# S5 fed by a planned clock, more modulation chunks beside it, four rotation tables made early: one core, two hybrid layers

## The chip, the cores and the metric

The kernel runs on one core of a Trainium2 chip. The metric is the device time of one execution in microseconds (us); before the change the median of three runs is 3060.22 us, the lowest 3058.78 us and the highest 3065.08 us. A profiled execution was taken apart from these.

## The reference

One inference step of a two-layer backbone over 128 context tokens and 128 latent tokens, with D = 2048, all in fp32. Each layer, cut to what matters:

```python
mod = silu(cond) @ w_mod[l] + b_mod[l]             # 6 vectors of 2048, for context and latent
h = rms_norm(x) * (1 + scale1) + shift1
q, k, v, xr, xg, us, gl = split(h @ w_in)          # gl: three gates of 2048
attn = block_attention(rope(norm(q)), rope(norm(k)), v)         # 8 heads, 2 kv heads
rec  = gelu(xg) * rg_lru_bidir(conv4(xr))                       # 1024 channels
ssm  = s5_bidir(us); ssm = gelu(ssm); ssm *= sigmoid(ssm @ glu_w)   # 64 groups, 64 complex states, 2 directions
merged = g0 * (attn @ w_pa) + g1 * (rec @ w_pr) + g2 * (ssm @ w_ps)
x = x + gate1 * (merged @ w_o)
a, b = split((rms_norm(x) * (1 + scale2) + shift2) @ w_up)
x = x + gate2 * ((gelu(conv3(a)) * b) @ w_down)
```

The S5 branch is a linear recurrence with complex coefficients, h[t] = A h[t-1] + B u[t], run forward and backward. The outputs are x of both token sets, the context's k and v, and the final states.

## The kernel before, in words

**Units.** All weights come from DRAM as half-tiles of 512 KB, called `raw` (a ring of six buffers, loaded by SP). fp32 products are made from two parts: ACT casts a half-tile to `whi` (`acp`, L114) and DVE subtracts to get `wlo` (L70). A unit is one 128-column output of a 2048-row product: two half-tiles, 32 matmuls on PE into `ps_mm` (L117); then ACT copies one half of the result and DVE adds the other (`pj`). So each unit asks DVE for two `wlo` of 128x1024 and one `pj` of 128x256.

**Items.** `run_items` walks a list: units ("w"), single steps ("do") and modulation loads ("mod"). A layer's list is: w_us, q, k, v, xr (the columns of w_in), then w_pa with the gate of the attention branch and the xg columns, then w_pr with its gates, the S5's glu, w_ps, w_o, and the FFN. Layer 0's w_us and half of its q are made in a startup stage beside the first norm.

**Modulation chunks.** The products with w_mod for later vectors are filler. `filler(n)` adds `MODR[seg]` per unit to a credit, and whenever this reaches 4 it puts a chunk of four w_mod half-tiles into the list. A chunk is four loads of 512 KB and 16 narrow matmuls into `ps_md` (two records each in the trace), with no split, so nothing for DVE or ACT but a small end. The six entries of `MODR` stand for six stretches of the program in turn.

**What runs beside the units.** Attention, the RG-LRU and the S5 are Python generators, and each `next` emits one step. `feed` (L215), called after every unit, steps them: attention four steps a unit (`RATT`), LRU 1.9, and the S5 by a budget of planned DVE time per unit, `RS5` = 4.2 us in layer 0 and 2.6 us in layer 1, cut to `SATT` = 2.2 and 1.5 us while attention runs. The planned cost of a DVE instruction is 150 or 90 ns plus a rate by its size.

**The S5.** Eight tiles, two directions each, so 16 passes a layer (`s5_gen`). A pass on DVE is two products `pa` and `pb` of PE's `ps_v` with a table of rotations, two sums into `xs`, a scan (L1001), two products back (`pc`, `pd`) and two sums into `H`. The table and the other coefficients of a tile stand in the buffer `blk` (two of them) and are made by `s5_prep` (L831) on DVE: the coefficients `S` and `cc`, and the table by six doublings. Layer 0's tiles 0 and 1 are prepared in the startup by `prep_step`, two steps per eighth of it; tiles 2 to 7 inside the S5 of layer 0. Layer 1's eight are prepared during layer 0's FFN and kept in DRAM (`s5a`, `s5v`).

**Order.** Each engine executes its instructions in the order that the framework's scheduler writes. It works from the order of emission, its own estimate of times and the free buffers. A buffer is named by its tag: `t` (products p1/p2 of the preparation), `S`, `xs`, `RH` and `H` have one buffer each or a pair.

Of the kernel before, what the change touches and what calls it, by code (L numbers as in the profile page):

```python
# [33 lines left out]
class Builder:  # L34
    RS5 = (4.2, 2.6)
    HLB = 3
    GS0 = 10
    PATIENCE = 3
    NRAW = 6
    AHEAD = 20  # L40
    MODR = (0.94, 0.94, 0.9, 0.9, 0.9, 1.44)
    RATT = (4.0, 4.0)
    RLRU = (1.9, 1.9)
    SATT = (2.2, 1.5)
# [209 lines left out]
    def run_items(self):  # L254
# [26 lines left out]
        for i in range(n):  # L281
# [15 lines left out]
            else:  # L297
# [21 lines left out]
                self.feed(1.0)  # L319
# [109 lines left out]
    def startup(self, begin, evs, begin2, evs2):  # L429
# [22 lines left out]
        prep = [self.s5_prep(0, 0), self.s5_prep(0, 1)]  # L452
# [58 lines left out]
        for q in range(8):  # L511
# [319 lines left out]
    def s5_prep(self, l, ft):  # L831
# [51 lines left out]
        self.add(cc[:, 1, 1], t1[:, 1], t2[:, 0])  # L883
        self.nc.vector.memset(tab[:, 0, :, 0:1], 1.0)
# [161 lines left out]
    def att_gen(self, l):  # L1046
        nc, d = self.nc, self.d
        Q, KV = self.Q, self.KVT
        KR, KA, VP, VS = (KV[n] for n in ("KR", "KA", "VP", "VS"))

# [19 lines left out]
        self.recip(sg, sg)  # L1070
        self.ts(sg, sg, float(P) ** -0.5, ALU.mult)
# [4 lines left out]
        qs = Q[:, :, P:T]  # L1076
        for g in range(3):
            n = 4 if g < 2 else 2
            src = qs[:, 4 * g:4 * g + 4, :] if g < 2 else KR[:, :, P:T]
            w = self.misc([4, P])  # L1080
            self.mm(w[:, 0:n, :], self.PERM, src, True, True)
            t1 = F1
            self.mul(t1[:, 0:n], src, self.COS[:, None, :].to_broadcast([P, n, P]))
            yield
            t2 = self.st("F2", [4, P], name="rt2")
            self.mul(t2[:, 0:n], w[:, 0:n], self.SIN[:, None, :].to_broadcast([P, n, P]))
            self.add(src if g < 2 else KA[:, :, P:T], t1[:, 0:n], t2[:, 0:n])
            yield
        for kv in range(2):
            for hh in range(4):  # L1090
                h = 4 * kv + hh
                s = self.misc([3, P])
                self.mm(s[:, 0, :], Q[:, h, 0:P], KR[:, kv, 0:P], True, True)
                self.mm(s[:, 1:3, :].rearrange("p a b -> p (a b)"), Q[:, h, P:T], KA[:, kv, :], True, True)
                yield
                sm = self.st("sm", [6], name="sm", bufs=2)
                nc.vector.tensor_reduce(sm[:, 0:1], s[:, 0, :], mybir.AxisListType.X, ALU.max)
                nc.vector.tensor_reduce(sm[:, 1:2], s[:, 1:3, :], mybir.AxisListType.XY, ALU.max)
                self.dve += 600
                sgh = sg[:, 2 * h:2 * h + 2]  # L1100
                self.stt(sm[:, 2:4], sm[:, 0:2], -1.0, sgh, ALU.mult, ALU.mult)
                p = F1[:, 0:3]
                self.act(p[:, 0, :], s[:, 0, :], AF.Exp, bias=sm[:, 2:3], scale=sgh[:, 0:1], accum=sm[:, 4:5])
                self.act(p[:, 1:3, :], s[:, 1:3, :], AF.Exp, bias=sm[:, 3:4], scale=sgh[:, 1:2], accum=sm[:, 5:6])
                yield
                self.recip(sm[:, 4:6], sm[:, 4:6])
                self.ts(p[:, 0, :], p[:, 0, :], sm[:, 4:5], ALU.mult)
                self.ts(p[:, 1:3, :], p[:, 1:3, :], sm[:, 5:6], ALU.mult)
                yield
                w = self.misc([3, P])  # L1110
                for j in range(3):
                    self.tr(w[:, j, :], p[:, j, :])
                yield
                self.acp(PT[:, :, hh, :], w)
            yield
            for s in range(2):
                o = self.misc([4, P])
                if s == 0:
                    self.mm(o, VP[:, kv * P:(kv + 1) * P], PT[:, 0], True, True)
                else:  # L1120
                    for j in range(2):
                        self.mm(o, VS[:, j, kv * P:(kv + 1) * P], PT[:, 1 + j], j == 0, j == 1)
                yield
# [7 lines left out]
    def lru_gen(self, l):  # L1131
        nc, d = self.nc, self.d
        XC = self.XC
        for k in range(8):
# [29 lines left out]
            for dd in range(2):  # L1164
                for s in range(2):
# [5 lines left out]
                    self.dve += 90 + 1.04 * P  # L1171
# [8 lines left out]
    def layer(self, l):  # L1180
# [71 lines left out]
        for g in range(2):  # L1252
            def mm(hv, g=g):
# [14 lines left out]
                if g == 1:  # L1268
                    def ev():
# [5 lines left out]
                        self.start(self.att, self.RATT[l], "att")  # L1275
# [343 lines left out]
def program(nc, shapes):  # L1619
# [30 lines left out]
```

## Time and profile before

| what | value |
|---|---|
| median of 3 runs | 3060.22 us |
| the profiled execution | 3068.35 us, its span 3066.6 us |
| PE (matmul) busy | 2952.2 us, 96% |
| PEld (weight load) busy | 2483.6 us, 81% |
| DVE busy | 2257.7 us, 74% |
| ACT busy | 1730.4 us, 56% |
| DMA read and written | 704.46 MB and 15.68 MB, 235 GB/s over the span |

The shares are of the span of the profiled execution. PE's share is an average over stretches in which it is nearly full and others in which it waits, so the table alone doesn't tell what a change in one stretch is worth. The stretches used below, in us from the span's start: 0 to 162 the startup; 162 to 307 the rest of q, k, v and xr of layer 0; 307 to 815 its w_pa and w_pr with gates; 815 to 1613 its glu, w_ps, w_o and FFN; 1613 to 2337 layer 1 up to its w_pr; 2337 to the end the rest of layer 1.

### The profile page before, as it was taken

How to read it: one execution, taken by the hardware profiler on the slowest of the kernel's cores; microseconds unless marked ns; L12 is line 12 of the kernel's file. 1: busy time of each engine (PE TensorE's matmuls, PEld its weight loads, DVE VectorE, ACT ScalarE, POOL GpSimd, SP SyncE). 2: the span in 40 equal slices, each digit the busy share in tenths (PEclk: the TensorE clock that was granted, in tenths of full speed). 3: DMA queues.
4: the chain of work that ended last, by engine and by line, in shares of the span. 5: the costliest groups of instructions: out<-in, count | busy, mean ns of one | idle time of the engine just before them, and what ended most of it. 6: DMA issues, size and time to landing. Idle time of an engine off the chain costs nothing.

```text
span 3066.6 us, 53452 instructions
## 1 busy us (share of the span) xinstructions
PE 2952.2 (96%) x20833; PEld 2483.6 (81%) x20833; DVE 2257.7 (74%) x4000; ACT 1730.4 (56%) x2914; POOL 45.9 (1%) x87
## 2 busy tenths in 40 slices
PE   6899999999999999999999999999999999999999
PEld 4787778777888888888887877777788888888888
DVE  6389899999576787787667788688755777666665
ACT  4355668745556745445566557676445567544553
POOL 0000000000000000000000000000000000000000
PEclk8999999999999999999999999999999999999999
DMA  9856566566777778778776777777776556555553
GB/s 382 306 183 203 177 208 218 196 208 236 263 262 253 251 282 286 273 270 291 266 275 241 267 250 252 244 259 250 261 278 202 178 175 208 197 187 192 181 197 132
DMA packets 188493, 723.64 MB, mean 236 GB/s; under 512 B 21520, under 2 KB 22064, under 8 KB 179280
## 3 DMA queue, kind: packets, MB, share of 16 engines
q1 hardware_dynamic: 180288, 689.86, 65.3%
q0 software_dynamic: 7664, 28.27, 2.5%
q8 instruction: 164, 2.69, 0.4%
q10 hardware_dynamic: 288, 2.10, 0.2%
q14 instruction: 89, 0.73, 0.1%
HBM read 704.46 MB, written 15.68 MB: 235 GB/s over the span
## 4 chain that ended last, share of the span: by engine, by line
PE 66%; DVE 14%; issue 9%; DMA 6%; ACT 5%; POOL 0%; DVEq 0%; ACTq 0%; SPq 0%; POOLq 0%
PE ps_mm L117 59%; DVE wlo L70 5%; DMA raw<-in_w_in 3%; PE ps_md L117 3%; ACT whi L114 2%; DVE xs L1001 2%; PE ps_aux L117 1%; PE ps_v L117 1%; DVE xs L70 1%; PE ps_y L117 1%; DVE t L70 1%; DVE pb L70 1%; DVE pj L70 1%; DMA raw<-in_w_mod 1%; DMA raw<-in_w_pr 1%
## 5 line engine op out<-in xcount | busy, mean ns | idle before, releaser
L117 PE MATMUL ps_mm<-h,whi 128*128 128x512 f32 (+1 forms) x4976 | 1743.9, 395 | 40.7 <-DVE pj L70 32.4
L70 DVE TENSOR_TENSOR wlo<-raw,whi 128x1024 fp32r<-128x1024 f32 x896 | 1095.3, 1223 | 449.4 <-ACT whi L114 444.7
L117 PE MATMUL ps_mm<-h,wlo 128*128 128x256 f32 x4912 | 1341.7, 283 | 17.1 <-DVE wlo L70 16.7
L114 ACT CAST whi<-raw 128x1024 fp32r<-128x1024 f32 x896 | 939.6, 1049 | 517.8 <-PE ps_mm L117 231.6
L117 PEld LDWEIGHTS ps_mm<-h,whi 128*128 128x128 f32 x4976 | 926.6, 190 | 254.1 <-DVE pj L70 39.7
L117 PEld LDWEIGHTS ps_mm<-h,wlo 128*128 128x128 f32 x4912 | 934.7, 190 | 44.6 <-DVE wlo L70 23.2
L114 ACT COPY pj<-ps_mm 128x256 f32<-128x256 f32 x479 | 176.1, 369 | 500.1 <-PE ps_mm L117 499.4
L117 PE MATMUL ps_mm<-hid,whi 128*128 128x512 f32 x1024 | 354.7, 393 | 0.0
L70 DVE TENSOR_TENSOR pj<-ps_mm,pj 128x256 f32<-128x256 f32 x479 | 200.9, 421 | 204.9 <-ACT pj L114 200.1
L117 PE MATMUL ps_mm<-br,whi 128*128 128x512 f32 x896 | 322.1, 402 | 12.3 <-DVE pj L70 12.3
L117 PE MATMUL ps_mm<-hid,wlo 128*128 128x256 f32 x1024 | 277.3, 281 | 0.0
L117 PE MATMUL ps_mm<-br,wlo 128*128 128x256 f32 x896 | 233.8, 281 | 0.0
L117 PEld LDWEIGHTS ps_mm<-hid,whi 128*128 128x128 f32 x1024 | 188.5, 188 | 39.5 <-issue 2.5
L117 PEld LDWEIGHTS ps_mm<-br,whi 128*128 128x128 f32 x896 | 165.4, 189 | 54.9 <-DVE pj L70 19.4
L117 PEld LDWEIGHTS ps_mm<-hid,wlo 128*128 128x128 f32 x1024 | 193.1, 189 | 5.4 <-DVE wlo L70 0.3
L117 PEld LDWEIGHTS ps_mm<-br,wlo 128*128 128x128 f32 x896 | 169.6, 189 | 8.4 <-ACT RH L110 0.4
L117 PE MATMUL ps_md<-raw,SC 128*32 128x256 f32 x2560 | 162.0, 381 | 0.0
L117 PEld LDWEIGHTS ps_md<-raw,SC 128*32 128x32 f32 x2560 | 82.9, 109 | 50.7 <-issue 12.6
L110 ACT ACT_TABLE_LOAD x90 | 115.5, 1283 | 10.3 <-DMA cv<-in_cT 5.0
L110 ACT ACTIVATE RH<-CST,TINY 128x256 f32<-128x256 f32 x128 | 57.2, 500 | 56.3 <-DVE xs L1001 56.1
L1001 DVE TENSOR_TENSOR_SCAN xs<-RH,xs 128x1056 f32<-128x1056 f32 x32 | 75.4, 2355 | 0.6
L83 DVE SCALAR_TENSOR_TENSOR x<-pj,MOD,x 128x128 f32<-128x128 f32 x192 | 59.0, 349 | 3.0
(239 smaller groups left out, 2448.4 us busy)
## 6 DMA issues: line engine op xcount, KB each, us to landing
raw<-in_w_mod SPq DMA_DIRECT2D x384, 512.0 KB, 6.9
raw<-in_w_in SPq DMA_DIRECT2D x304, 512.0 KB, 4.9
raw<-in_w_up SPq DMA_DIRECT2D x166, 512.0 KB, 4.4
raw<-in_w_up SPq DMA_DIRECT2D x45, 1024.0 KB, 4.9
raw<-in_w_down SPq DMA_DIRECT2D x90, 512.0 KB, 4.3
raw<-in_w_o SPq DMA_DIRECT2D x64, 512.0 KB, 4.4
raw<-in_w_down SPq DMA_DIRECT2D x19, 1024.0 KB, 4.9
raw<-in_w_pa SPq DMA_DIRECT2D x32, 512.0 KB, 4.6
```

The source lines that it names most:

```text
L70: self.nc.vector.tensor_tensor(out=out, in0=a, in1=b, op=op)
L83: self.nc.vector.scalar_tensor_tensor(out=out, in0=a, scalar=s, in1=b, op0=op0, op1=op1)
L110: self.nc.scalar.activation(out, a, func, **k)
L114: self.nc.scalar.copy(out, a)
L117: self.nc.tensor.matmul(out, lhsT, rhs, start=start, stop=stop, **k)
L1001: nc.vector.tensor_tensor_scan(out=x, data0=r, data1=x, initial=0.0, op0=ALU.mult, op1=ALU.add)
```

## The change

The S5 is no longer fed at a fixed rate. The planner now keeps a planned clock for DVE and one for PE; after every unit the S5 is stepped as long as DVE's clock is behind PE's plus `LEAD` (4.2 us in layer 0, 3.0 us in layer 1). The planned costs are closer to the measured ones (65 ns instead of 150 or 90). Attention takes one longer step per half unit, and within a kv head the scores of one head are emitted before the previous head's result is copied. `MODR` puts more chunks into the first stretch (1.5 instead of 0.94) and, per unit, fewer into the later ones. The rotation tables of layer 0's tiles 2 to 5 are made in the startup's list by `s5_tab_store`, in the buffers `xs`, `RH` and `H`, and stored by POOL to a DRAM tensor `s5t` (532 KB each); `s5_prep` then loads them by SP.

```diff
-    RS5 = (4.2, 2.6)
+    LEAD = (4200, 3000)
     HLB = 3
     GS0 = 10
+    NTAB = 4
     PATIENCE = 3
     NRAW = 6
     AHEAD = 20
-    MODR = (0.94, 0.94, 0.9, 0.9, 0.9, 1.44)
-    RATT = (4.0, 4.0)
+    MODR = (1.5, 0.6, 0.65, 0.65, 0.65, 1.2)
     RLRU = (1.9, 1.9)
-    SATT = (2.2, 1.5)
     NE = (3, 3)
     PA = 1
...
-        self.dve += 150 + 1.04 * out.free_size()
+        self.dve += 65 + 1.04 * out.free_size()
...
+        n, m = rhs.free_size(), lhsT.free_size()
+        if rhs.dtype == F32R:
+            self.pe += 7 + 0.443 * n
+        else:
+            self.pe += max(1.69 * n, 220) / (4 if m == 32 else 1)
...
+        self.tsplit = self.clock()
...
+        self.feed_att()
+
+    def clock(self):
+
+        self.dvet += self.dve - self.dve0
+        self.dve0 = self.dve
+        return self.dvet
+
+    def feed(self):
+
+        for g in sorted(self.gens, key=lambda g: g[3] == "s5"):
+            if g[3] == "att":
+                continue
             s5 = g[3] == "s5"
-            g[2] += w * (self.SATT[self.lay] if att and s5 else g[1])
+            g[2] = 0 if s5 else g[2] + g[1]
             if g[4] is not None:
                 g[4] += 1
-            while g[2] >= (0 if s5 else 1) and g in self.gens:
+            while g in self.gens and (self.clock() < self.pe + self.LEAD[self.lay] if s5 else g[2] >= 1):
                 if g[4] is not None and g[4] < self.PATIENCE:
-                    g[2] = min(g[2], 1.0)
                     break
-                t = self.dve
+                g[2] -= 1
                 self.step(g)
-                g[2] -= (self.dve - t) / 1e3 if s5 else 1
+
+    def feed_att(self):
+        for g in list(self.gens):
+            if g[3] == "att":
+                self.step(g)
...
-            if g[4] is not None:
+            if g[4]:
...
+                self.pe = max(self.pe, self.tsplit - 1200)
...
+                self.dvet = max(self.clock(), self.pe)
...
-                self.feed(1.0)
+                self.feed_att()
+                self.feed()
...
-        prep = [self.s5_prep(0, 0), self.s5_prep(0, 1)]
+        prep = [self.s5_prep(0, 0), self.s5_prep(0, 1)] + [self.s5_tab_store(2 + k) for k in range(self.NTAB)]
...
-            for _ in range(2):
+            for _ in range((2, 2, 3, 4, 5, 6, 7)[q - 1]):
                 self.do(prep_step)
         self.items += [us[7], qs[3]]
+        self.do(lambda: [0 for p in prep for _ in p])
...
+        if l == 0 and 2 <= ft < 2 + self.NTAB:
+            nc.sync.dma_start(tab.rearrange("p c d n -> p (c d n)"), d["s5t"][ft])
+            yield
+        else:
+            yield from self.s5_tab(tab, ft)
+
+    def s5_tab(self, tab, ft):
...
+    def s5_tab_store(self, ft):
+        t = self.st(("xs", "RH", "H")[ft % 3], [2, 8, 65], name="tb")
+        yield from self.s5_tab(t, ft)
+        self.nc.gpsimd.dma_start(self.d["s5t"][ft], t.rearrange("p c d n -> p (c d n)"))
...
-            for hh in range(4):
-                h = 4 * kv + hh
-                s = self.misc([3, P])
-                self.mm(s[:, 0, :], Q[:, h, 0:P], KR[:, kv, 0:P], True, True)
-                self.mm(s[:, 1:3, :].rearrange("p a b -> p (a b)"), Q[:, h, P:T], KA[:, kv, :], True, True)
+            for hh in range(5):
+                if hh:
+                    w = turn()
+                if hh < 4:
+                    s = scores(4 * kv + hh)
+                if hh:
+                    self.acp(PT[:, :, hh - 1, :], w)
...
-                    self.start(self.s5, self.RS5[l], "s5")
+                    self.start(self.s5, 0, "s5")
...
-                        self.start(self.att, self.RATT[l], "att")
+                        self.start(self.att, 1.0, "att")
```

What moves on the engines, from the order in which they execute. First DVE at the end of the startup, before the change; `S` is the coefficient tile of the second S5 tile, `u` the S5's input, `t_...` the products of the preparation.

```order
L70 TENSOR_TENSOR wlo<-raw,whi 128x1024 x6
L94 COPY u<-usn 32x4x128 x4
L88 TENSOR_SCALAR PK_67<-PK_67 128x64
L70 TENSOR_TENSOR wlo<-raw,whi 128x1024
L94 COPY u<-usn 32x4x128 x4
L70 TENSOR_TENSOR wlo<-raw,whi 128x1024
L70 TENSOR_TENSOR S<-t_1003,t_1004 128x2x4x32 x2
L70 TENSOR_TENSOR wlo<-raw,whi 128x1024
L70 TENSOR_TENSOR t_1009<-S,TINY 128x2x128
```

The same place after the change.

```order
L72 TENSOR_TENSOR wlo<-raw,whi 128x1024 x6
L96 COPY u<-usn 32x4x128 x4
L90 TENSOR_SCALAR PK_67<-PK_67 128x64
L72 TENSOR_TENSOR wlo<-raw,whi 128x1024
L96 COPY u<-usn 32x4x128 x4
L72 TENSOR_TENSOR wlo<-raw,whi 128x1024
L72 TENSOR_TENSOR S<-t_868,t_869 128x2x4x32 x2
L72 TENSOR_TENSOR t_1008<-S,TINY 128x2x128
L72 TENSOR_TENSOR t_1009<-S,TINY 128x2x128
```

Up to the second tile's `S` the rows are the same: no product of the four tables (`tb`) stands among the startup's splits.

DVE further on, after the change: the end of the second tile's own table, and the first rows of the four new ones.

```order
L72 TENSOR_TENSOR wlo<-raw,whi 128x1024
L72 TENSOR_TENSOR blk<-t_1242,t_1243 128x8x32 x2
L72 TENSOR_TENSOR wlo<-raw,whi 128x1024
L72 TENSOR_TENSOR t_1252<-tb 128x16
L72 TENSOR_TENSOR t_1253<-tb 128x16
L72 TENSOR_TENSOR tb<-t_1252,t_1253 128x8 x2
L72 TENSOR_TENSOR t_1258<-tb 128x16x2
```

The `tb` tables begin here, behind the startup's last splits and the second tile's coefficients.

DVE where the first S5 pass begins, before the change (`pa`, `pb`, `xs` are its first instructions, and the scan is the row on L1001).

```order
L70 TENSOR_TENSOR blk<-t_1383,t_1384 128x8x32 x2
L70 TENSOR_TENSOR wlo<-raw,whi 128x1024
L70 TENSOR_TENSOR pa<-ps_v,blk 128x1024
L70 TENSOR_TENSOR pb<-ps_v,blk 128x1024
L70 TENSOR_TENSOR pj<-ps_mm,pj 128x256
L70 TENSOR_TENSOR xs<-pa,pb 128x4x2x64 x2
L70 TENSOR_TENSOR wlo<-raw,whi 128x1024
L1001 SCALAR_TENSOR_TENSOR xs<-RH,xs 128x1056
```

And after the change (the scan is on L1038).

```order
L996 MEMSET RH 128x16
L72 TENSOR_TENSOR tb<-t_1723,t_1724 128x8x16 x2
L72 TENSOR_TENSOR t_1729<-tb 128x512
L72 TENSOR_TENSOR t_1730<-tb 128x512
L72 TENSOR_TENSOR tb<-t_1729,t_1730 128x8x32 x2
L72 TENSOR_TENSOR wlo<-raw,whi 128x1024
L72 TENSOR_TENSOR pa<-ps_v,blk 128x1024
L72 TENSOR_TENSOR pb<-ps_v,blk 128x1024
L72 TENSOR_TENSOR wlo<-raw,whi 128x1024
L72 TENSOR_TENSOR xs<-pa,pb 128x4x2x64 x2
L72 TENSOR_TENSOR wlo<-raw,whi 128x1024
L1038 SCALAR_TENSOR_TENSOR xs<-RH,xs 128x1056
```

The first pass stands right behind the second tile's table before, and behind all four `tb` tables and the clearing of `RH` now; in rows it begins at 239 before and at 337 now.

SP's loads from the end of the startup, before the change (`in_w_in` and `in_w_v` are weights of units, `in_w_mod` those of chunks).

```order
L178 DMA raw<-in_w_in 128x1024 x5
L178 DMA raw<-in_w_mod 128x1024 x4
L178 DMA raw<-in_w_in 128x1024 x2
L178 DMA raw<-in_w_v 128x1024 x4
L178 DMA raw<-in_w_in 128x1024 x2
L178 DMA raw<-in_w_mod 128x1024 x4
L178 DMA raw<-in_w_in 128x1024 x8
L178 DMA raw<-in_w_mod 128x1024 x4
L178 DMA raw<-in_w_in 128x1024 x10
L178 DMA raw<-in_w_mod 128x1024 x4
```

And after it.

```order
L186 DMA raw<-in_w_in 128x1024 x6
L186 DMA raw<-in_w_mod 128x1024 x4
L186 DMA raw<-in_w_v 128x1024 x4
L186 DMA raw<-in_w_mod 128x1024 x4
L186 DMA raw<-in_w_in 128x1024 x6
L186 DMA raw<-in_w_mod 128x1024 x4
L186 DMA raw<-in_w_in 128x1024 x6
L910 DMA blk<-s5t 128x1040
L186 DMA raw<-in_w_mod 128x1024 x4
L186 DMA raw<-in_w_in 128x1024 x4
L186 DMA raw<-in_w_mod 128x1024 x4
```

Chunks stand closer together, and the first load of a stored table stands in the same queue as the weights.

POOL's queue behind the loads of the cached k and v, after the change; in the order before, the fourth `bp` load stands here directly behind `in_cv`.

```order
L1263 DMA kv<-in_ck 128x2x128
L1264 DMA kv<-in_cv 128x256
L939 DMA s5t<-tb 128x1040 x4
L1317 DMA out_new_v<-kv 128x256
L1148 DMA out_new_k<-kv 256x1x128
L861 DMA blk<-in_cp 128x512
L859 DMA bp<-in_bp 128x512
L1181 DMA gw<-in_gw 128x512
L859 DMA bp<-in_bp 128x512
```

The third tile's loads (`blk<-in_cp` and the `bp` behind the two outputs) now wait behind the four stores of tables.

## Rows read from the trace of the kernel before

**Rows 1.** Busy time by stretch: from:to, length, engines, TensorE clock, DMA.
```profile
core 0: us, PE busy (x) PEld busy (x) DVE busy (x) ACT busy (x) POOL busy (x), PEclk, DMA share, GB/s
0.00:162.00 162.00, 125.32 (x1167) 97.59 (x1167) 85.74 (x263) 72.87 (x154) 4.30 (x11) 0.94 0.88 336
162.00:307.00 145.00, 139.30 (x1081) 118.10 (x1079) 128.91 (x252) 80.33 (x146) 2.85 (x5) 0.99 0.59 193
307.00:815.00 508.00, 474.81 (x3613) 393.38 (x3612) 443.18 (x849) 318.28 (x506) 12.38 (x23) 0.97 0.64 214
815.00:1613.00 798.00, 796.02 (x5493) 673.08 (x5491) 576.55 (x1085) 429.86 (x730) 16.27 (x30) 1.00 0.77 269
1613.00:2337.00 724.00, 694.85 (x5294) 571.49 (x5291) 531.66 (x796) 433.42 (x732) 8.46 (x15) 0.99 0.73 254
2337.00:3066.60 729.60, 721.91 (x4200) 629.98 (x4198) 491.63 (x758) 395.65 (x648) 1.62 (x3) 1.00 0.56 184
```
**Rows 2.** Chain of waits in the FFN of layer 0: start, us, what.
```profile
1184.24 22.46 PE ps_mm L117 x128
1206.70 1.86 PE ps_md L117 x32
```
**Rows 3.** Matmuls of chunks in 162:815, 815:1613, 1613:2337: count, ns least/median/most.
```profile
L117 PE MATMUL ps_md<-raw,SC x608: 377/379/404, 199.7 to 798.1; 128*32 128x256 f32 x152
L117 PE MATMUL ps_md<-raw,SC x928: 377/379/404, 820.9 to 1594.5; 128*32 128x256 f32 x186
L117 PE MATMUL ps_md<-raw,SC x1024: 377/379/404, 1619.7 to 2285.8; 128*32 128x256 f32 x171
```
**Rows 4.** Busy time of the preparation's `t`, one table's stretch: DVE (count).
```profile
171.70:182.60 10.90, 5.80 (x24) 1.00 0.48 144
```
**Rows 5.** Groups on DVE in 162:815: count | busy us, mean ns | idle before.
```profile
L1001 DVE TENSOR_TENSOR_SCAN xs<-RH,xs 128x1056 f32<-128x1056 f32 x16 | 37.7, 2354 | 0.2
L70 DVE TENSOR_TENSOR H<-pc,pd 128x520 f32<-128x520 f32 x32 | 21.5, 695 | 0.0
L70 DVE TENSOR_TENSOR xs<-pa,pb 128x512 f32<-128x512 f32 x32 | 21.0, 687 | 0.1
L70 DVE TENSOR_TENSOR pc<-xs,blk 128x1040 f32<-128x1040 f32 x16 | 19.8, 1238 | 0.2
L70 DVE TENSOR_TENSOR pa<-ps_v,blk 128x1024 f32<-128x1024 f32 x16 | 19.6, 1222 | 0.6
L70 DVE TENSOR_TENSOR S<-t,t 128x256 f32<-128x256 f32 x32 | 12.5, 421 | 0.2
L70 DVE TENSOR_TENSOR t<-blk,TINY 128x512 f32<-128x512 f32 x16 | 10.5, 688 | 10.4 <-DMA blk<-in_cp 10.3
```
**Rows 6.** Busy time of the softmax's `sm` in 162:307: DVE, ACT.
```profile
162.00:307.00 145.00, 10.68 (x42) 7.68 (x28) 0.99 0.59 193
```
**Rows 7.** Busy time of `ps_mm` alone in 307:815: PE, PEld, DVE, ACT.
```profile
307.00:815.00 508.00, 390.62 (x2111) 329.65 (x2111) 33.47 (x81) 29.48 (x81) 0.97 0.64 214
```
**Rows 8.** Waits in 162:815: waiting line, awaited: us in total, times, longest.
```profile
DVE wlo L70 <- ACT whi L114: 52.5, 46, 3.9
ACT whi L114 <- DMA raw<-in_w_in: 51.2, 37, 4.1
PE ps_mm L117 <- DVE pj L70: 24.4, 14, 3.9
```
**Rows 9.** Waits in 1613:2337.
```profile
ACT whi L114 <- DMA raw<-in_w_in: 66.2, 53, 5.2
PE ps_mm L117 <- DVE pj L70: 18.1, 11, 4.6
ACT whi L114 <- DMA raw<-in_w_pr: 11.2, 9, 2.9
```
**Rows 10.** Transfers to and from the stored S5 tiles: count, KB, us to landing.
```profile
s5v<-vs POOLq DMA_DIRECT2D x8, 512.0 KB, 5.2
s5a<-blk POOLq DMA_DIRECT2D x8, 808.0 KB, 9.3
```

More of the change, by code (lines that the diff above doesn't have):

```diff
@@ L51, in __init__ @@
         self.act_t = 0.0
+        self.pe = 0.0
+        self.dve0 = 0.0
+        self.dvet = 0.0
         self.pending = []
@@ L81, in stt @@
     def stt(self, out, a, s, b, op0, op1):
-        self.dve += 90 + 1.04 * out.free_size() + (0 if isinstance(s, (int, float)) else 63)
+        self.dve += 65 + 1.04 * out.free_size() + (0 if isinstance(s, (int, float)) else 63)
         self.nc.vector.scalar_tensor_tensor(out=out, in0=a, scalar=s, in1=b, op0=op0, op1=op1)
@@ L887, in s5_prep @@
         self.cp(tab[:, :, :, 1], e1)
-        yield
         n = 1
@@ L1049, in att_gen, with rope, scores, softmax @@
         KR, KA, VP, VS = (KV[n] for n in ("KR", "KA", "VP", "VS"))
+        rq = self.QR
+        F4 = self.st("F4", [4, 4, P], name="attf")
+        F1, PT = F4[:, 3], F4[:, 0:3]
+        qs = Q[:, :, P:T]
+        def rope(g):
+            n = 4 if g < 2 else 2
+            src = qs[:, 4 * g:4 * g + 4, :] if g < 2 else KR[:, :, P:T]
+            w = self.misc([4, P])
+            self.mm(w[:, 0:n, :], self.PERM, src, True, True)
+            t1, t2 = F1, self.st("F2", [4, P], name="rt2")
+            self.mul(t1[:, 0:n], src, self.COS[:, None, :].to_broadcast([P, n, P]))
+            self.mul(t2[:, 0:n], w[:, 0:n], self.SIN[:, None, :].to_broadcast([P, n, P]))
+            self.add(src if g < 2 else KA[:, :, P:T], t1[:, 0:n], t2[:, 0:n])
+        def scores(h):
+            kv = h // 4
+            s = self.misc([3, P])
+            self.mm(s[:, 0, :], Q[:, h, 0:P], KR[:, kv, 0:P], True, True)
+            self.mm(s[:, 1:3, :].rearrange("p a b -> p (a b)"), Q[:, h, P:T], KA[:, kv, :], True, True)
+            return s
+        def softmax(h, s):
+            sm = self.st("sm", [6], name="sm", bufs=2)
+            nc.vector.tensor_reduce(sm[:, 0:1], s[:, 0, :], mybir.AxisListType.X, ALU.max)
+            nc.vector.tensor_reduce(sm[:, 1:2], s[:, 1:3, :], mybir.AxisListType.XY, ALU.max)
+            self.dve += 600
+            sgh = sg[:, 2 * h:2 * h + 2]
+            self.stt(sm[:, 2:4], sm[:, 0:2], -1.0, sgh, ALU.mult, ALU.mult)
+            p = F1[:, 0:3]
+            self.act(p[:, 0, :], s[:, 0, :], AF.Exp, bias=sm[:, 2:3], scale=sgh[:, 0:1], accum=sm[:, 4:5])
+            self.act(p[:, 1:3, :], s[:, 1:3, :], AF.Exp, bias=sm[:, 3:4], scale=sgh[:, 1:2], accum=sm[:, 5:6])
+            self.recip(sm[:, 4:6], sm[:, 4:6])
+            self.ts(p[:, 0, :], p[:, 0, :], sm[:, 4:5], ALU.mult)
+            self.ts(p[:, 1:3, :], p[:, 1:3, :], sm[:, 5:6], ALU.mult)
+        def turn():
+            w = self.misc([3, P])
+            for j in range(3):
+                self.tr(w[:, j, :], F1[:, j, :])
+            return w
         m = self.misc([4])
@@ L1062, in att_gen @@
         sg = self.st("sg", [16], name="sg")
-        self.act(sg, ql, AF.Sqrt, bias=self.EPST, scale=1.0 / P)
+        self.act(sg, rq.rearrange("p a b -> p (a b)"), AF.Sqrt, bias=self.EPST, scale=1.0 / P)
+        self.recip(rc, rc)
+        self.recip(sg, sg)
+        self.ts(sg, sg, float(P) ** -0.5, ALU.mult)
         yield
-        self.recip(rc, rc)
         rk = self.misc([2, T])
@@ L1075, in att_gen @@
         yield
-        qs = Q[:, :, P:T]
         for g in range(3):
[L1078 to L1087, printed above, removed]
+            rope(g)
@@ L1115, in att_gen @@
-            yield
-            for s in range(2):
[L1117 to L1123, printed above, removed]
+            for hh in range(5):
[5 more added lines that the diff above has]
+                    self.acp(PT[:, :, hh - 1, :], w)
+                if hh < 4:
+                    softmax(4 * kv + hh, s)
+                yield
@@ L1124, in att_gen @@
+            o = [self.misc([4, P]) for _ in range(2)]
+            self.mm(o[0], VP[:, kv * P:(kv + 1) * P], PT[:, 0], True, True)
+            for j in range(2):
+                self.mm(o[1], VS[:, j, kv * P:(kv + 1) * P], PT[:, 1 + j], j == 0, j == 1)
+            for s in range(2):
                 hi = self.BR[kv][:, :, 0, s * P:(s + 1) * P]
                 lo = self.BR[kv][:, :, 1, s * P:(s + 1) * P]
-                self.acp(hi, o)
-                self.sub(lo, o, hi.bitcast(F32))
+                self.acp(hi, o[s])
+                self.sub(lo, o[s], hi.bitcast(F32))
```

36 lines of the change are left out of this document (5 added, 31 removed).

## The prediction

> **What bounds the kernel now.** I read the busy times by stretch first [rows 1]; the reader is to compare PE and DVE with the length of each stretch. From 815 to 1613 PE is busy 796.0 of 798 us: PE alone sets the time, and DVE (576.6) has room. In the startup neither is full and the DMA share is 0.88: transfers lead. In the three stretches with S5 and attention beside the units, nothing is full: 162 to 307 has DVE at 128.9 of 145 us (89%) and PE at 139.3; 307 to 815 DVE at 443.2 of 508 (87%) and PE at 474.8; layer 1's 1613 to 2337 DVE at 531.7 of 724 (73%) and PE at 694.9. There the two take turns at waiting: in 162 to 815 `wlo` waits 52.5 us for `whi`, `whi` 51.2 us for its load, PE's units 24.4 us for DVE's `pj` [rows 8]. DVE is late in one place and idle in the next.
>
> The chain of waits gives PE's pace where it sets the time: 22.46 us for 128 matmuls, which is four units, so 5.615 us a unit; a modulation chunk between them takes 1.86 us [rows 2]. `ps_md` counts the chunks: 608, 928 and 1024 records in three stretches, at 32 a chunk 19, 29 and 32 [rows 3].
>
> **The change part by part.** The sum is made against the profiled execution, 3068.35 us (span 3066.6 and 1.75 around it). That is 8.1 above the median of 3060.22, and I take 8.1 off at the end. What moves where I counted in the order of DVE and PE, between the splits that both kernels have in common.
>
> (a) 162 to 307. The order puts all four tables here; two were computed here before by that count and five are now, the four and tile 1's. So three are added. A table is 24 instructions, 5.80 us [rows 4]: 3 x 5.80 = 17.4. One more S5 pass is scanned, by rows 5: pa and pb 2 x 1.22, xs 2 x 0.69, the scan 2.35, pc and pd 2 x 1.24, H 2 x 0.70, together 10.0; and one further pa and pb, 2.4. Three more heads of softmax: 42 instructions of seven heads take 10.7 [rows 6], so 3 x 1.53 = 4.6. One more tile's coefficients, about ten of 0.421 and four of 0.688 [rows 5], 7.0. Sum 41.4; DVE's work becomes 128.9 + 41.4 = 170, more than the stretch is long. If all of today's idle 16 us is filled, the stretch lengthens by 25; if DVE's share stays at 89%, by 170 / 0.889 - 145 = 46. I take +30, nearer the lower end: the tables wait for no other engine. The 46 stays as a bound.
>
> (b) 307 to 815. The same 41 us leave (three tables, a pass, the heads and a tile's coefficients), so DVE's work falls to 402, 79% of 508, like layer 1's 73%. What is late next is PE, which also gets 7 of the 9 chunks that are added in 162 to 815 (19 become 28). By today's busy time: 474.8 + 7 x 1.86 = 488, so 20 can be gained. That busy time holds `ps_mm` stretched by waits: 390.6 [rows 7] for 66 units, where 66 x 5.615 = 371 would do; then PE needs 468 and 40 can be gained. I take -24, near the row as it stands, because the last part of the S5 doesn't come sooner: by the order its sixteenth scan stands behind 48 of w_pr's 68 half-units, at 41 of 68 before. Bounds -20 and -40; DVE's own bound is farther, 402 at today's share of 87% would make 461, -47.
>
> (c) 815 to 1613. Eight chunks fewer (29 become 21). PE is full here and nothing takes their place: 8 x 1.86 = -14.9. This term is the surest; if loads set the pace between chunks it could only be more, and the stretch's 0.77 DMA share falls with it.
>
> (d) Layer 1. From 1613 to 2337 four chunks fewer (32 become 28), -7.4, if PE sets the end there, and nothing if DVE or the loads do; behind 2337, where PE is busy 721.9 of 729.6, three chunks more, +5.6. S5 and attention keep their work and only move: by the count 12 us of DVE's work are added up to 1845, 22 leave 1845 to 2109, and 10 are added behind. I take -1.8 for the layer; an even feed could return up to half of the 29 us that PE doesn't work there (-14), and the raw loads' waits stay as they are.
>
> (e) The small edits. The planned costs change only where steps are emitted, and that is counted in (a), (b) and (d). SP issues four table loads of 532 KB in line with the raw loads; its stored tiles of layer 1, 808 KB, take 9.3 us out and 512 KB 5.2, so about 5.4 us for a table by its size, hidden by the six raw buffers and by the pass before it; cost 0, and 4 x 5.4 = 22 us if each held `whi` up for all of its time. POOL now stores four tables ahead of `out_new_v`, `out_new_k` and the third tile's `bp`; POOL works 15 of the 653 us in these two stretches, and what waits is the third tile's preparation, one to two passes from being needed: 0. The clearing of `xs` and `RH` in front of the first pass waits until the tables in these buffers are stored (5.2 us for 512 KB [rows 10]); behind that wait on DVE are the next `wlo`, so up to 5 us, part of (a)'s 30.
>
> By the Trainium skill ("Perfetto Trace Analysis", section "Identifying the Most-Contended Engine") one judges the vector engine by its busy time and the tensor engine by its weight loads, and improves the most contended. Its reading here: DVE 572.1 of 653 us from 162 to 815, 88%, weight loads 511.5, 78% [rows 1]; DVE's work there is only moved, so (a) and (b) together would give 0 and the sum would be -14.9 - 1.8 = -16.7, that is 3043.5. The trace agrees that DVE is the fuller of the two, but not that DVE alone sets the time, since `wlo` waits 52.5 us there [rows 8]. This lies within the forecast's own range.
>
> The sum: +30 - 24 - 14.9 - 1.8 = -10.7, so 3057.6 for a profiled execution and 3049.5 against the median.
>
> **The rivals.**
>
> R1, slower: the tables plug the S5. No product of a table comes in front of the second tile's `S`; all four stand between tile 1's table and the first pass (rows 239 and 337 of the order). DVE is handed 23 us of table work there in one piece, at a place where it is already the fuller engine, `pj` and `wlo` queue behind it, and PE waits. (a) is then +46, (b) -20: 46 - 20 - 14.9 - 1.8 = +9.3, 3069.5. And the chunks come closer together, four raw buffers each: `whi` waits 77.4 us for loads with 32 chunks (66.2 and 11.2 [rows 9]) and 51.2 with 19 [rows 8], so 2.0 us a chunk, 18 for nine more; with half of it on the path 3078. I give it 3074. It decides when the first stretch lengthens by more than (b) gives back plus 17. For it: DVE's 89%. Against it: the splits stand between the tables' rows, nine half-tiles of them, so PE isn't cut off.
>
> R2, faster: the planned clock really evens DVE. (a) at its lower bound, +25, (b) at -40, (c) and (d) as above: -31.7, 3028.5; with (d)'s -14 about 3016. For it: `wlo` waits 52.5 us in 162 to 815 for no lack of DVE time [rows 8], and a fixed budget can't use these. Against it: the first of these waits is for `whi` and its load, which no S5 step shortens.
>
> R3, no change: what (c) saves is paid in layer 0, whose PE takes nine more chunks, 16.7 us. (a) + (b) = +15 or so gives -2 in all, 3058; for it speaks that chunks are only moved, 80 before and 80 after, and that PE was 94% busy where they go (614.1 of 653 us [rows 1]).
>
> That the change doesn't do what it says holds for one part: the tables do not stand beside the first norm; the forecast counts them where they stand.
>
> **How the numbers follow.** The forecast 0.36, with its own range of 3040 to 3054; R1 0.25; R2 0.20; R3 0.19. Under 0.2% of 3060.22, 6.1 us, this kernel's measurement can't tell a difference. Faster is R2 and the forecast but for 0.03 at its upper edge: 0.53; same is R3 and these 0.03: 0.22; slower 0.25. The range reaches from R2 with layer 1's share, 3015, to R1's 3074 and a little, 3076.
>
> **What would show it.** (a) the first S5 scan comes some 25 us later than before and the stretch up to xr's end takes 170 to 190 us, DVE over 90% in it. (b) w_pa and w_pr with their gates take 468 to 490 us. (c) 815 to 1613 becomes 783 us long, with 672 `ps_md` records. (d) 896 records in layer 1's first stretches. Wrong would be: a first stretch that grows by less than 25 (the tables found idle time), or by more than 46; waits of `whi` for `raw` in layer 0 clearly over 69 us; a layer 1 that moves by more than 14 either way, which nothing in this sum would explain.

## The result and the profile after

The changed kernel takes 3089.38 us (median of 4 runs, 3084.57 to 3093.19), the kernel before on the same chip 3059.5. The ratio over the runs is 1.0087, with a 95% interval of 1.0071 to 1.0103 (the two medians alone would give 1.0098): slower, and outside the range that was forecast. In e2 and in e7 below, one of ten executions ran at a lower clock (3659.47 and 3226.08 us), and the ratios leave it out.

The profiled execution has a span of 3090.0 us, 23.4 more than that of before; the medians are 29.9 apart, since the profiled execution of before was a long one (3068.35 us). Executions of one kernel differ by some 10 us (19 of the kernel before, beside e9 to e12, lie between 3053.51 and 3067.03), so a few us in one stretch of one profile tell nothing.

To compare stretches, the cuts are put where PE begins the same unit in each kernel: at the 193rd, 801st, 2913th, 7009th and 10113th matmul of the units (`ps_mm`). In the kernel before that is, to within half a us, at the cuts of [rows 1]. The second cut is w_pa's first matmul, which reads `br`; before the change it starts at 306.7 us and after it at 347.5, the first start in each row:

```profile
L117 PE MATMUL ps_mm<-br,whi x896: 387/395/632, 306.7 to 2430.3; 128*128 128x512 f32 x180
```
```profile
L124 PE MATMUL ps_mm<-br,whi x896: 387/395/628, 347.5 to 2453.6; 128*128 128x512 f32 x180
```

The view of [rows 1], of the changed kernel:

```profile
core 0: us, PE busy (x) PEld busy (x) DVE busy (x) ACT busy (x) POOL busy (x), PEclk, DMA share, GB/s
0.00:164.20 164.20, 127.23 (x1167) 99.39 (x1167) 85.69 (x267) 71.30 (x150) 4.29 (x11) 0.92 0.87 331
164.20:347.50 183.30, 160.69 (x1241) 129.09 (x1239) 164.47 (x363) 89.78 (x167) 6.08 (x11) 0.93 0.58 201
347.50:852.60 505.10, 478.17 (x3743) 394.54 (x3742) 411.90 (x737) 309.49 (x490) 11.30 (x21) 0.98 0.71 244
852.60:1636.50 783.90, 780.54 (x5232) 663.53 (x5230) 575.30 (x1081) 429.32 (x730) 16.27 (x30) 1.00 0.73 251
1636.50:2352.60 716.10, 688.82 (x5162) 566.72 (x5158) 530.58 (x793) 427.26 (x726) 8.47 (x15) 0.99 0.71 245
2352.60:3090.00 737.40, 728.98 (x4300) 633.47 (x4298) 491.47 (x761) 397.02 (x649) 1.61 (x3) 1.00 0.57 191
```

Against [rows 1] the startup is 2.2 us longer and the first stretch 38.3; w_pa and w_pr are 2.9 shorter, the FFN of layer 0 14.1 and layer 1 7.9; the end is 7.8 longer. That is the whole +23.4. The chunks stand where the order said; here are the five counts that answer to [rows 3], from 164.2, 347.5, 852.6, 1636.5 and 2352.6 on:

```profile
L124 PE MATMUL ps_md<-raw,SC x192: 377/379/404, 189.1 to 328.5; 128*32 128x256 f32 x192
L124 PE MATMUL ps_md<-raw,SC x704: 377/379/636, 354.0 to 824.4; 128*32 128x256 f32 x176
L124 PE MATMUL ps_md<-raw,SC x672: 377/379/404, 858.3 to 1629.5; 128*32 128x256 f32 x168
L124 PE MATMUL ps_md<-raw,SC x896: 377/379/636, 1657.0 to 2333.6; 128*32 128x256 f32 x180
L124 PE MATMUL ps_md<-raw,SC x96: 379/379/403, 2358.3 to 2399.0; 128*32 128x256 f32 x96
```

At 32 a chunk these are 6, 22, 21, 28 and 3. Of the 19 that the first two stretches had before, 4 stood in the first and 15 in w_pa and w_pr. Now the S5's first scans, in the kernel before and in the changed one (least, median and longest time, then first and last start):

```profile
L1001 DVE TENSOR_TENSOR_SCAN xs<-RH,xs x4: 2351/2356/2357, 188.7 to 307.1; 128x1056 f32<-128x1056 f32 x4
```
```profile
L1038 DVE TENSOR_TENSOR_SCAN xs<-RH,xs x4: 2346/2349/2358, 236.0 to 300.4; 128x1056 f32<-128x1056 f32 x4
```

The first scan comes 47 us later. What follows it is seen in slices of 10 us of the changed kernel (columns as above):

```profile
220.00:230.00 10.00, 5.49 (x58) 3.84 (x56) 7.30 (x28) 4.14 (x9) 0.85 (x2) 0.98 0.71 267
230.00:240.00 10.00, 9.60 (x51) 8.16 (x52) 10.00 (x10) 3.73 (x7) 0.57 (x2) 0.67 0.91 307
240.00:250.00 10.00, 10.00 (x88) 7.81 (x88) 10.00 (x15) 4.09 (x6) 0.00 (x0) 1.00 0.32 128
250.00:260.00 10.00, 9.07 (x113) 5.80 (x111) 10.00 (x19) 4.71 (x8) 1.79 (x3) 1.00 0.63 212
260.00:270.00 10.00, 5.67 (x35) 4.73 (x35) 9.35 (x18) 2.87 (x4) 0.00 (x0) 0.86 0.57 224
270.00:280.00 10.00, 3.61 (x17) 2.73 (x14) 10.00 (x14) 1.74 (x5) 0.00 (x0) 0.50 0.08 24
```

From 230 to 280 DVE is full. PE runs dry behind 260: it is busy 5.7 and 3.6 of 10 us in the last two slices, and in the last the granted clock is 0.50, the lower of the two levels. DVE's groups from 230 to 285 say what it is full of:

```profile
L72 DVE TENSOR_TENSOR wlo<-raw,whi 128x1024 fp32r<-128x1024 f32 x10 | 12.1, 1216 | 0.0
L1038 DVE TENSOR_TENSOR_SCAN xs<-RH,xs 128x1056 f32<-128x1056 f32 x3 | 7.0, 2348 | 0.0
```

Ten splits in 55 us, enough for five units of 5.6 us; between them stand three S5 passes, and the work of xr's convolution, of attention and of the third tile. The tables pushed the S5 back, and it then catches up in front of the splits.

### The profile page after: what moved, and what is told of

It is laid out like the page before. It is cut to its first block, busy times and chain, and to the rows that moved or that the text cites. A ratio compares the mean times of both kernels' runs of the same rounds, so it can differ in the third digit from the quotient of the medians.

```text
span 3090.0 us, 53468 instructions
## 1 busy us (share of the span) xinstructions
PE 2964.4 (96%) x20833; PEld 2486.7 (80%) x20833; DVE 2259.4 (73%) x4000; ACT 1724.2 (56%) x2908; POOL 48.0 (2%) x91
## 4 chain that ended last, share of the span: by engine, by line
PE 68%; DVE 12%; DMA 7%; issue 6%; ACT 6%; POOL 0%; SPq 0%; ACTq 0%; DVEq 0%; POOLq 0%
PE ps_mm L124 61%; DVE wlo L72 4%; DMA raw<-in_w_in 4%; PE ps_md L124 3%; ACT whi L116 3%; PE ps_aux L124 2%; DVE xs L1038 1%; PE ps_v L124 1%; ACT ltmp L112 1%; DMA raw<-in_w_mod 1%; PE ps_y L124 1%; DVE xs L72 1%; DVE pb L72 1%; DVE pj L72 1%; DVE t L72 1%
## 5 line engine op out<-in xcount | busy, mean ns | idle before, releaser
L124 PE MATMUL ps_mm<-h,whi 128*128 128x512 f32 (+1 forms) x4976 | 1747.4, 396 | 32.6 <-DVE pj L72 18.6
L72 DVE TENSOR_TENSOR wlo<-raw,whi 128x1024 fp32r<-128x1024 f32 x896 | 1094.6, 1222 | 478.1 <-ACT whi L116 465.0
L1038 DVE TENSOR_TENSOR_SCAN xs<-RH,xs 128x1056 f32<-128x1056 f32 x32 | 75.3, 2353 | 0.7
```

The costliest lines, as they stand in the source:

```text
L1038: nc.vector.tensor_tensor_scan(out=x, data0=r, data1=x, initial=0.0, op0=ALU.mult, op1=ALU.add)
```

## The experiments

All times are ratios to the kernel before on the same chip. The two parts of the change that can be taken out singly, chunks and tables, give a square, and e4 adds the chunks on the old feed.

| ratio (95% interval) | chunks of before | new chunks |
|---|---|---|
| kernel before | 1 | e4: 1.0032 (1.0016 to 1.0047) |
| new feed and attention, no tables | e3: 0.9921 (0.9902 to 0.9940) | e1: 1.0024 (1.0010 to 1.0037) |
| the same with tables | e2: 0.9993 (0.9983 to 1.0003) | the change: 1.0087 (1.0071 to 1.0103) |

The spans of the profiled executions, cut as above:

| us | startup | first stretch | w_pa, w_pr | FFN | layer 1 | rest | span |
|---|---|---|---|---|---|---|---|
| before | 162.0 | 145.0 | 508.0 | 798.0 | 724.0 | 729.6 | 3066.6 |
| the change | 164.2 | 183.3 | 505.1 | 783.9 | 716.1 | 737.4 | 3090.0 |
| e1, no tables | 163.7 | 158.2 | 507.5 | 784.5 | 718.6 | 736.9 | 3069.4 |
| e2, old chunks | 160.2 | 174.0 | 478.1 | 799.7 | 715.4 | 730.5 | 3057.9 |
| e3, neither | 160.2 | 151.5 | 482.2 | 800.1 | 710.4 | 730.0 | 3034.4 |
| e4, chunks alone | 159.6 | 152.2 | 516.1 | 788.6 | 716.7 | 740.8 | 3074.0 |
| e5, e1 with seven buffers | 163.8 | 157.9 | 501.0 | 779.9 | 693.8 | 738.1 | 3034.5 |
| e6, e3 with seven buffers | 164.7 | 154.0 | 482.3 | 795.8 | 703.3 | 730.0 | 3030.1 |
| e8, attention alone | 161.3 | 152.1 | 496.4 | 799.3 | 725.3 | 730.0 | 3064.4 |
| e9, tables not made | 165.6 | 151.5 | 483.0 | 798.8 | 718.0 | 730.2 | 3047.1 |
| e10, the change with seven | 162.0 | 179.6 | 504.8 | 780.2 | 695.2 | 738.4 | 3060.2 |
| e11, tables first, seven | 168.7 | 152.3 | 476.0 | 796.3 | 703.4 | 730.3 | 3027.0 |
| e12, clock alone | 164.3 | 148.0 | 502.1 | 798.1 | 725.4 | 730.0 | 3067.9 |

**e1, no tables.** 

```diff
-    NTAB = 4
+    NTAB = 0
-            for _ in range((2, 2, 3, 4, 5, 6, 7)[q - 1]):
+            for _ in range(2):
```

Expected: 

> The changed kernel without the four early tables: they are computed in s5_prep again and the startup has its two steps per eighth. Theory T (the tables stand between the startup and the first S5 pass, hold xs, RH and H until they are stored, and the S5 then catches up back to back on DVE while PE starves): the first pass comes back to about 184 us, startup plus first stretch lose most of their +28, and the whole takes 3061 to 3068. Theory C (the nine chunks more in layer 0 are what is paid): 3084 to 3092, as the changed kernel. Theory F (the clock-fed S5 itself floods DVE): 3078 to 3090, with stretches of DVE at 10 of 10 us and PE below 6 of 10 still there.

Measured 3071.27 us, 1.0024. Theory T named the place: the first scan is back at 192.0 us, the first stretch falls from 183.3 to 158.2, and no other moves by more than 3. The total stays over T's 3061 to 3068, since the rest is not the tables'. Theories C and F as the only cause, with 3078 and more, fall.

**e2, the chunks of before.** 

```diff
-    MODR = (1.5, 0.6, 0.65, 0.65, 0.65, 1.2)
+    MODR = (0.94, 0.94, 0.9, 0.9, 0.9, 1.44)
```

Expected: 

> The changed kernel with the MODR of before, so chunks stand as before and tables, feed and attention are the new ones. Theory C: w_pa and w_pr lose the 13 us of seven chunks and the waits for loads that come with them, 307 to 815 of before comes to about 495 instead of 518, the FFN takes 798 again: 3075 to 3084. Theory T: the first stretch stays some 25 longer than before, the FFN's 19 us come back: 3085 to 3095.

Measured 3063.38 us, 0.9993: below both theories. The chunks cost more than either said. With those of before, w_pa and w_pr take 478.1 us instead of 505.1 and the first stretch 174.0 instead of 183.3; layer 1, which has four chunks more, is as long as in the change (715.4 and 716.1).

**e3, both taken back** (the edits of e1 and e2 together). Expected: 

> The changed kernel without tables and with the MODR of before: only the S5's feed by clock, the planned costs and the attention in longer steps are left. Theory T: 3053 to 3065, within 0.2% of before or a little faster. Theory F: 3070 to 3085, the first stretch over 160 us.

Measured 3040.11 us, 0.9921: feed and attention are a clear gain, which neither theory had. The first stretches of e2 and of e3 show the tables' price:

```profile
160.20:334.20 174.00, 155.66 (x1178) 124.62 (x1175) 162.31 (x361) 89.42 (x167) 6.11 (x11) 0.95 0.54 177
```
```profile
160.20:311.70 151.50, 148.19 (x1178) 121.29 (x1175) 142.12 (x285) 88.32 (x161) 3.95 (x7) 1.00 0.56 180
```

With tables DVE has 20 us more to do, the stretch is 22.5 longer, PE idles 18.3 instead of 3.3 us and its clock falls from 1.00 to 0.95. Now w_pa and w_pr of e3 and of e1, which differ in chunks alone: windows, and the waits of ACT's cast for loads.

```profile
311.70:793.90 482.20, 463.61 (x3521) 385.97 (x3518) 428.16 (x817) 306.65 (x489) 11.34 (x21) 0.98 0.67 226
```
```profile
ACT whi L116 <- DMA raw<-in_w_in: 33.4, 22, 3.9
ACT whi L116 <- DMA raw<-in_w_pa: 2.3, 2, 1.2
ACT whi L116 <- DMA raw<-in_w_pr: 2.0, 2, 1.5
```
```profile
321.90:829.40 507.50, 476.16 (x3792) 392.56 (x3790) 435.43 (x828) 312.68 (x495) 11.88 (x22) 0.99 0.71 241
```
```profile
ACT whi L116 <- DMA raw<-in_w_in: 71.1, 44, 4.8
ACT whi L116 <- DMA raw<-in_w_pr: 12.2, 8, 3.1
ACT whi L116 <- DMA raw<-in_w_pa: 8.1, 8, 2.2
```

Fifteen chunks stand here in e3 and 22 in e1. Seven more lengthen the stretch by 25.3 us, 3.6 each, where their matmuls are 7 x 1.86 = 13.0; PE idles 31.3 instead of 18.6 us, and the casts wait for loads 91.4 instead of 37.7.

**e4, the chunks alone** (the kernel before with the new `MODR`). Expected: 

> The kernel before with the new MODR alone. Theory C: what the FFN saves (19 us) is paid in layer 0 (17 us of matmuls and the waits for loads) and behind 2337 (5.6): 3060 to 3072. Theory T: the chunks fall into PE's idle time there in part, 3045 to 3056.

Measured 3073.79 us, 1.0032: theory C, a little above its range. The FFN gives 9.4 back, layer 1 7.3 and the startup 2.4; the first stretch, w_pa and w_pr together pay 15.3, the end 11.2.

**e5 and e6, seven raw buffers** with the new chunks (as e1) and with those of before (as e3).

```diff
-    NRAW = 6
+    NRAW = 7
```

Expected of e5: 

> The new chunks without the early tables, as e1, with seven raw buffers instead of six. Theory L (a chunk's four loads fill the ring of raw buffers, so that the next units' half-tiles come late: whi waited 91 us for raw in w_pa and w_pr of e1, 38 in e3): the price of the new chunks, 31 to 35 us between e3 and e1, falls by a third or more against e6, and whi's waits for raw in that stretch fall under 70 us. Theory P (a chunk takes PE's time and nothing else): the difference between this and e6 stays at 28 to 35.

Expected of e6: 

> As e3 (feed and attention alone, chunks and tables of before), with seven raw buffers. Theory L: 3030 to 3038, some us under e3's 3040. Theory P: e3's 3040 within 3.

Measured 3038.90 us, 0.9924 (0.9900 to 0.9947), and 3030.47, 0.9889 (0.9857 to 0.9920). The chunks' price falls from 1.03% to 0.35%: theory L. The waits for loads in w_pa and w_pr of e5:

```profile
ACT whi L116 <- DMA raw<-in_w_in: 15.4, 13, 3.6
```

But the stretches say something else on the place than L did. That wait fell from 91.4 to 15.4 us, and w_pa and w_pr of e5 still take 501.0 us, only 6.5 less than in e1. Here are w_pa and w_pr of e6 and of e5:

```profile
318.70:801.00 482.30, 461.42 (x3521) 385.79 (x3518) 428.62 (x817) 306.65 (x490) 11.31 (x21) 0.99 0.68 226
```
```profile
321.70:822.70 501.00, 475.48 (x3792) 395.26 (x3791) 433.79 (x828) 310.31 (x495) 11.84 (x22) 0.99 0.72 244
```

The seven chunks still cost 18.7 us here, 14.1 of PE's busy and 4.6 of its idle time. Most of the gain, 17.7 of 30.6 us by the spans, is in layer 1; its stretch in e6 and in e5:

```profile
1596.80:2300.10 703.30, 688.47 (x5291) 568.76 (x5288) 531.86 (x796) 425.83 (x729) 8.46 (x15) 1.00 0.75 261
```
```profile
1602.60:2296.40 693.80, 680.92 (x5162) 565.09 (x5159) 530.37 (x793) 422.89 (x726) 8.46 (x15) 1.00 0.74 253
```

With seven buffers four chunks fewer shorten layer 1 by 9.5 us. With six they lengthened it by 8.2 (e3 to e1), and on the old feed they shortened it by 7.3 (before to e4); these runs don't show why.

**e7, the tables ahead of the second tile**, with the chunks of before (as e2 otherwise).

```diff
-        prep = [self.s5_prep(0, 0), self.s5_prep(0, 1)] + [self.s5_tab_store(2 + k) for k in range(self.NTAB)]
+        prep = [self.s5_prep(0, 0)] + [self.s5_tab_store(2 + k) for k in range(self.NTAB)] + [self.s5_prep(0, 1)]
```

Expected: 

> The tables and the new feed with the MODR of before, as e2, but the four tables are emitted ahead of the second tile's preparation; in the order of DVE all of them then stand among the startup's splits, and the second tile's preparation in front of the first pass. Theory T (where the tables stand makes their price): startup at most 5 us longer, first stretch 135 to 145 instead of 158, w_pa and w_pr not longer than in e2: 3030 to 3045. If instead the table loads, the stores or the buffers make the price: 3055 to 3066 as e2.

Measured 3049.64 us, 0.9951 (0.9934 to 0.9968): between the two. The place makes 0.42 of the tables' 0.72%. e2 and e7 ran on different chips, each against its own runs of the kernel before. Only the times of e7 are used.

**e8, the attention alone.** The planner's clock is taken out again: the S5 has the rates, the cuts beside attention and the planned costs of before; attention keeps its longer steps. The test in `visit` is that of before.

```diff
-            while g in self.gens and (self.clock() < self.pe + self.LEAD[self.lay] if s5 else g[2] >= 1):
+            g[2] += self.SATT[self.lay] if busy and s5 else g[1]
...
+            while g[2] >= (0 if s5 else 1) and g in self.gens:
```

Expected: 

> The kernel before with the attention in longer merged steps alone; the S5 has its fixed rates and planned costs of before, chunks and tables are those of before. If e3's gain of 0.8% comes from the attention: 3034 to 3046. If it comes from the S5's feed by clock: 3054 to 3068.

Measured 3062.33 us, 0.9985 (0.9967 to 1.0002): next to nothing, and the interval holds 1.

**e9, the tables not made**, with stores, loads and buffers kept (as e2 otherwise). The buffers are filled with ones at the start, so the stores too come early.

```diff
-        yield from self.s5_tab(t, ft)
+        self.nc.vector.memset(t, 1.0)
+        for ns in (1890, 1059, 1857):
+            self.dve += ns
+            yield
```

Expected: 

> As e2 (tables, new feed, MODR of before), but the four tables' doublings are left out: each buffer is filled with ones by one instruction at the start, stored by POOL and loaded as before, and the planner still counts the tables' time. So layer 0's tiles 2 to 5 work with wrong rotations. What is left is the stores, the loads and the held buffers; what is gone is 23 us of DVE work. If DVE's work between startup and first pass is the price of the tables: 3025 to 3040, a little under e3 (its 17 to 23 us of work are gone altogether). If the held buffers, stores or loads are: 3050 to 3065 as e2.

Measured 3046.75 us, 0.9954 (0.9939 to 0.9969): again between. The first stretch is back at e3's 151.5 us. What is left against e3, 0.33%, stands in the profiles mostly in the startup (165.6 us instead of 160.2) and in layer 1 (718.0 instead of 710.4), which has no such table. The startup's part isn't clear of chance: without early stores it took from 159.6 to 164.7. The four stores, issued at the start, run beside the first weights:

```profile
0.00:165.60 165.60, 123.81 (x1167) 96.08 (x1167) 88.63 (x267) 72.15 (x153) 6.48 (x15) 0.95 0.90 341
```
```profile
s5t<-tb POOLq DMA_DIRECT2D x4, 520.0 KB, 13.3
```

A store takes 13.3 us (median) to land there and 4.5 in the changed kernel. By the Trainium skill ("DMA: Bandwidth & Descriptors", section "Issuing engines are not separate DMA queues") transfers issued on different engines share the same 16 DMA engines and interleave. These two numbers agree: on POOL's queue a store lands later where the weights of SP's keep the DMA engines busy (a share of 0.90 here, 0.58 in the change's first stretch). What the stores cost the weights, no run here shows.

**e10, the whole change with seven buffers.** Expected: 

> The changed kernel with seven raw buffers, nothing else. If the prices of tables and of chunks add up as they did with six (tables +0.6 to 0.7%, chunks with seven +0.35%): 3055 to 3065, as before the change. If the tables need the loads too and their price falls with the ring: 3040 to 3050.

Measured 3061.41 us, 0.9996 (0.9983 to 1.0009): the prices add up. The tables still cost 0.72% (e5 to e10), the first stretch 179.6 us against 157.9. w_pa and w_pr take 504.8 us, as in the change (505.1), although the casts there wait for loads 4.8 us in place of 73.9.

**e11, the tables first, chunks of before, seven buffers.** Expected: 

> As e7 (the tables ahead of the second tile's preparation, MODR of before) with seven raw buffers. If tables that stand in the startup save DVE time in layer 0 once loads don't hold it: 3018 to 3028, under e6's 3030. If not: 3034 to 3045.

Measured 3027.91 us, 0.9886 (0.9868 to 0.9904), at the edge of the first range, level with e6, and the fastest of all; its startup:

```profile
0.00:168.70 168.70, 127.29 (x1166) 99.32 (x1167) 108.23 (x370) 73.27 (x154) 6.49 (x15) 0.91 0.88 340
```

Here the tables do stand beside the first norm: DVE is busy 22 us more in the startup than in e6 (108.2 and 85.8), which is 4 us longer; w_pa and w_pr are 6.3 shorter. Their gain is what the startup gives up, about nothing.

**e12, the clock alone.** The kernel of e3 with the attention of before, four short steps after each unit, and with the test in `visit` of before. Expected: 

> The kernel before with the S5 fed by the planned clock alone: attention in its four short steps a unit, chunks and tables of before. With e3 at 0.992 and e8 (attention alone) at 0.9985: if the clock makes e3's gain by itself, 3038 to 3050; if it needs the attention's longer steps, 3055 to 3066.

Measured 3072.62 us, 1.0038 (1.0025 to 1.0050): slower than before. So neither the clock nor the longer attention steps (e8) gain alone, and e3, which has both, gains 0.8%: in w_pa and w_pr (25.8 us shorter than before; e8 11.6, e12 5.9) and in layer 1 (13.6 shorter; e8 and e12 1 longer). Why they need each other was not followed further. The new test in `visit` (`if g[4]`) is in e3 and in neither of these two, so that it has no part in the gain is not shown.

## Why the prediction was wrong

The step that failed is **(b)**: "What is late next is PE, which also gets 7 of the 9 chunks"; "I take -24". It came out at -2.9. The relief was there: DVE's work fell by 31 us (443.2 [rows 1] to 411.9), and with the chunks of before w_pa and w_pr took 478.1 us, 29.9 less (e2). But the chunks were charged at their matmuls, 1.86 us each [rows 2], 13 us in all, with PE's waiting time as cover ("so 20 can be gained"). The seven cost 27.0 us there (e2 to the change), 3.9 each. PE's idle time was 33.2 us before, 17.9 in e2 and 26.9 in the change: the chunks didn't fall into idle time, they made more of it. So 14 of the 21 us by which (b) missed are the chunks', and 7 are relief that was counted and didn't come.

How much falls to (a) and how much to (b) hangs on the cut. Before the change, w_pa's first unit stands still halfway while the last heads of attention are finished; the second unit starts at 327.2 us, in the change at 355.9. Cut there, the first stretch grew by 26.5 and (b) is +8.6. (b) fails either way, and the chunks cost 26.6 there (e2 to the change).

Where the 14 come from is shown only in part. The waits of [rows 8] looked like the sign. In w_pa and w_pr alone `whi` waited 46.4 us for loads before the change, the sum of the first and the last row here, and `wlo` 40.8 for `whi`:

```profile
ACT whi L114 <- DMA raw<-in_w_in: 42.5, 32, 3.1
...
DVE wlo L70 <- ACT whi L114: 40.8, 36, 3.3
...
ACT whi L114 <- DMA raw<-in_w_pr: 3.9, 2, 2.2
```

In the change it is 73.9, the sum of the last three rows here, and 64.2:

```profile
DVE wlo L72 <- ACT whi L116: 64.2, 55, 5.5
ACT whi L116 <- DMA raw<-in_w_in: 58.6, 41, 3.7
...
ACT whi L116 <- DMA raw<-in_w_pr: 11.6, 7, 4.0
...
ACT whi L116 <- DMA raw<-in_w_pa: 3.7, 4, 1.9
```

With that, the prediction's own sign, waits of `whi` over 69 us in layer 0, was met. I had read that wait as 2.0 us a chunk (1.7 with the 3.9 for w_pr, which [rows 8] leave out), priced it in R1 alone, and at half. But a seventh buffer takes these waits away, and the stretch gets 6.5 us shorter without tables (e1 to e5) and not at all with them (the change to e10). So these waits are at most a part of what the chunks cost in this stretch beyond their matmuls; the rest of the cause stays open.

**(a)** was +30 with bounds of 25 and 46; the stretch grew by 38.3 and the startup by 2.2. The working holds: DVE's work there rose by 35.6 us where 41.4 was counted, and its share stayed at 89.7% (164.47 of 183.3), the case that was given as the upper bound. "The tables wait for no other engine", the reason for the lower end, missed who waits for them: the first scan came 47 us late, not 25, PE ran dry, and its clock fell from 0.99 to 0.93. The tables are 25.1 of the 38.3 (e1 to the change). Another 6.7 come with the two chunks more of this stretch (e3 to e1), which (a) did not charge, and 6.5 with feed and attention (before to e3).

**(c)** was -14.9 and came out at -14.1: right. **(d)** was -1.8 and came out at -0.1, with layer 1 at -7.9 and the end at +7.8 where -7.4 and +5.6 were worked out. For layer 1 some of that is luck: the same four chunks fewer gave from -9.5 to +8.2 in the pairs above. **(e)** charged the stored tables nothing: e9, with none of their DVE work, is still 0.33% over e3, and where that stands is not explained. A table is 520 KB in the unit of the views, not 532; its store took 4.5 us and its load 5.9, near the 5.4 that was worked out. ACT's first write of `RH` waited 7.3 us for a store, where up to 5 was allowed.

Of the rivals, R1 had the right sign, and the plug at the right place; its condition was met, a first stretch longer by 38.3 us against the 2.9 that (b) gave back plus 17. With (b) at -20 it came to 3074. R2's even feed is real only together with the longer attention steps (e3: 0.9921, e12: 1.0038); it was hidden by the two other parts. By the Trainium skill's rule on the most contended engine ("Perfetto Trace Analysis", section "Identifying the Most-Contended Engine"), as the prediction read it, the 653 us from 162 to 815 would have stayed; they became 688.4, so it was no nearer than (a) and (b) with their +6.

In sum: feed and attention -0.8%, chunks +0.9 to 1.0%, tables +0.6 to 0.7%, together +0.87% measured. The forecast set a gain of 39 us, in (b) and in the FFN's chunks, against the tables' 30. The FFN's part came; most of (b)'s went to the chunks.

## What to carry to other kernels

Charge filler work with more than its engine time where the engine already waits: here 1.86 us of matmuls cost 3.6 to 3.9 us a chunk in the stretch that took them. A longer ring of load buffers can make the same move cheap (1.03% to 0.35%), and not where the waits for loads stood. Work that is moved "early" stands where its buffers and its priority put it, so look at the order for the first instruction that has to stand behind it, and price the lateness of that one. When a change has several parts, take each out singly before judging any: here the gain of one was hidden by the prices of two.

## What was not expected of the hardware

Nothing is new in kind. In size: PE's granted clock was 0.50 in the slice from 270 to 280 us, in which it was busy 3.6 us, and the store of one 520 KB table took 13.3 us in the startup of e9, three times its 4.5 in the change.
